# A hybrid decoder trunk on one core: the planner's instruction order tied down by order-only edges

## The chip, the cores and the metric

The kernel runs on one core of one Trainium2 chip. A core has five engines that each work through an instruction stream of their own: PE (TensorE, matrix products; its weight loads are listed apart as PEld), DVE (VectorE), ACT (ScalarE), POOL (GpSimd) and SP (SyncE, which here issues most of the transfers). An engine takes its instructions strictly in the order of its stream; an instruction that has to wait for another engine or for a transfer holds up all that stand behind it. The metric is the device time of one execution in microseconds, the median of several.

## The reference

Two layers over 512 rows of 1024 numbers in float32. Each layer has three sub-layers, each with a normalisation ahead of it and one behind it:

```python
for i in range(2):
    h = rmsnorm(x, mix_pre_g[i])
    z = h @ w_in[i]                    # 1024 -> 3206, split into ten parts
    out_a = spatial_gating(...)        # 4 groups of 64, chunks of 128 rows
    out_b = retention_chunkwise(...)   # 6 heads of 64, rotary
    out_c = forgetting_attention(...)  # 6 heads of 64, blocks of 128 queries
    x = x + rmsnorm(concat(out_a, out_b, out_c) @ w_o[i], mix_post_g[i])

    h = rmsnorm(x, ffn_pre_g[i])
    g = causal_conv3(h @ w_gate[i])    # 1024 -> 4096
    f = (gelu(g) * (h @ w_up[i])) @ w_down[i]
    x = x + rmsnorm(f, ffn_post_g[i])

    gate = sigmoid(rmsnorm(x, ple_pre_g[i]) @ w_ple_gate[i])
    x = x + rmsnorm((p[i] @ w_ple_proj[i]) * gate, ple_post_g[i])
```

## The kernel before

**Products.** Every float32 operand is split into a high and a low part of the matmul type: `split` has ACT copy the high part and DVE subtract it from the source, which gives the low part. A product is then three matmuls (high by high, high by low, low by high; `mm3`). Row-major weights come through `tm_units`: a transfer on SP's queue into `traw`, then the split into `thl` (high and low side by side), two rows of blocks at a time.

**Start of the program.** Chunk 0 of the input `x` (128 rows) is loaded, and `Plain.__call__` prepares it for the products: DVE multiplies each half row by the gain into `h`, PE transposes the four 128x128 blocks of `h` into `hps` (a matmul with `k_ident`), and `split` stores them into `hT`. Then the weights of the projection `uv` are loaded and split, and chunks 1 to 3 are prepared in the same way. The projection takes 24 matmuls of 512 columns for each chunk, 96 in all, from `thl` and `hT` into `ps`. The next projection of the program, `fv`, has 390 columns a chunk, and its `thl` splits are 128x2x390.

**Mixers.** A written order of steps interleaves the three mixers. The last pair of heads of the forgetting attention, `fox_attend(2)`, ends in 10 matmuls `ops<-fet`, whose operand `fet` ACT and DVE copy out of PSUM; the result goes to `cc`. Behind it comes the last retention step and the out projection (`wo`, with weights in `thl` again, and the embedding's operands in `ehl`).

**Feed-forward.** 32 blocks a layer (`gate_up`), each 128 columns of four quarters of the weights. Seven products a block are taken from sums of the weights that DVE builds (`ws`, then the splits `wg`, `wsa`, `wsb`, `wu`); the results collect in the banks `beta` and `ag`, and DVE and ACT combine them in `gs` and `us`. Between these PE takes the matmuls of the down projection (`dn`) of an earlier group of blocks.

**What sets the order.** All calls go through the class `Plan`, which records them first. `issue()` then runs through the recorded program with costs of its own for each instruction, takes on each engine the first recorded one that is ready, and so gets one list, `order`. The instructions are made in that order. In the kernel before, the framework's own scheduler still gets the instructions after that and puts each engine's stream in order by its own rules, with only the true dependences as its limits; the streams that run are therefore not quite the list. All instructions are made at one line, so that every row of the profile has line 404.

Of the kernel before, what the change touches and what calls it, by code (L numbers as in the profile page):

```python
# [49 lines left out]
class Plan:  # L50
# [15 lines left out]
    HOP = {"PE": 197, "DVE": 128, "ACT": 131, "POOL": 80, "SP": 0}  # L66
    HOP_PE = {"PE": 0, "DVE": 250, "ACT": 270, "POOL": 190, "SP": 100}

    def __init__(self):
        self.ops = []  # L70
        self.table = {}
        self.tiles = {}
        self.real = {}
        self.fenced = False
        self.kind = {}
        self.place = {}
        self.scratch = bacc.Bacc("TRN2", target_bir_lowering=False, num_devices=1)
# [143 lines left out]
    def issue(self):  # L221
# [35 lines left out]
        order = []  # L257
# [52 lines left out]
        def unpark(tag, now):  # L310
            q = parked[tag]
            while q:
                other = blocked(q[0])
                if other == tag:
                    return
                i = heapq.heappop(q)
                if other is None:
                    take(i, now)
                else:
                    heapq.heappush(parked[other], i)  # L320

        def complete(i, now):
            nonlocal front
            freed = []
            for t in set(ops[i][5]):
                uses[t] -= 1
                if not uses[t]:
                    tag = self.tiles[t][0]
                    heapq.heappush(slots[tag], now)
                    if t in self.kind:  # L330
                        c, k = self.place[t]
                        heapq.heappush(unused[c], (now, k))
                        freed += [f"b8 {k}" for k in (*self.SETS, None)]
                    freed.append(tag)
            for j in users[i]:
                if ops[j][0] != "PE":
                    release(j, now)
                elif ops[i][0] != "PE":
                    release(j, now + self.HOP_PE[ops[i][0]] - self.HOP[ops[i][0]])
            done[i] = True  # L340
            if i == front:
                while front < n and done[front]:
                    front += 1
                freed = list(parked)
            for tag in freed:
                unpark(tag, now)

        def release(j, now):
            left[j] -= 1
            ready_at[j] = max(ready_at[j], now)  # L350
            if not left[j]:
                offer(j, now)
# [6 lines left out]
        while len(order) < n:  # L359
            progress = False  # L360
            for e in names:
                while waiting[e] and waiting[e][0][0] <= now:
                    _, pr, i = heapq.heappop(waiting[e])
                    heapq.heappush(ready[e], (pr, i))
                if ready[e] and free[e] <= now:
                    _, i = heapq.heappop(ready[e])
                    busy, nbytes = ops[i][6][:2]
                    if e == "PE":
                        if columns.get(now // self.TICK - 1, 0) < self.WARM:
                            busy *= 2  # L370
                        tick = (now + busy) // self.TICK
                        columns[tick] = columns.get(tick, 0) + ops[i][6][2]
                    if self.table.get(i) not in (None, table):
                        table = self.table[i]
                        busy += self.LOAD
                    free[e] = now + busy
                    end = now + busy + self.HOP[e]
                    if nbytes:
                        rate, wait = (215.0, 4500) if e == "POOL" else (340.0, 2600)
                        dma_free = max(dma_free, now + busy) + nbytes / rate  # L380
                        end = dma_free + wait
                    order.append(i)
                    heapq.heappush(finish, (end, i))
                    if e == "PE":
                        for j in users[i]:
                            if ops[j][0] == "PE":
                                release(j, now + busy)
                    progress = True
            if progress:
                continue  # L390
            nxt = [finish[0][0]] if finish else []
            for e in names:
                if ready[e]:
                    nxt.append(free[e])
                elif waiting[e]:
                    nxt.append(max(free[e], waiting[e][0][0]))
            t = min(x for x in nxt)
            now = max(now, t)
            while finish and finish[0][0] <= now:
                _, i = heapq.heappop(finish)  # L400
                complete(i, now)
        for i in order:
            o = ops[i]
            o[1](*[self.map(v) for v in o[2]], **{k: self.map(v) for k, v in o[3].items()})  # L404


def two_pi_parts():
# [66 lines left out]

def body(ctx, tc, a, out):
    nc = tc.nc
    plan = Plan()
    V, A, G, T, SY = (plan.engine(n, e) for n, e in (
        ("DVE", nc.vector), ("ACT", nc.scalar), ("POOL", nc.gpsimd), ("PE", nc.tensor), ("SP", nc.sync)))

# [39 lines left out]
    class Rows:  # L520
        def __init__(self, src):
            self.src, self.t = src, [None, None]
# [782 lines left out]
```

## Time and profile before

| | |
|---|---|
| median of 3 runs | 1635.08 us (1634.15 to 1640.05) |
| the profiled execution's own time | 1635.78 us |
| its span in the profile | 1633.7 us |
| mean granted TensorE clock | 0.995 of full speed |
| busy: PE, DVE, ACT, POOL | 98%, 76%, 51%, 6% of the span |

The own time is the span and 2.1 us around it. A busy share is a mean over the span; stretches with other limits lie inside it. In the views, an instruction's idle time before it is given with the engine whose signal ended it. A group "x24" in a timeline is 24 instructions of the same kind in a row. The three shapes on a row are partitions by elements.

### The profile page before, as it was taken

How to read it: one execution, taken by the hardware profiler on the slowest of the kernel's cores; microseconds unless marked ns; L12 is line 12 of the kernel's file. 1: busy time of each engine (PE TensorE's matmuls, PEld its weight loads, DVE VectorE, ACT ScalarE, POOL GpSimd, SP SyncE). 2: the span in 40 equal slices, each digit the busy share in tenths (PEclk: the TensorE clock that was granted, in tenths of full speed). 3: DMA queues.
4: the chain of work that ended last, by engine and by line, in shares of the span. 5: the costliest groups of instructions: out<-in, count | busy, mean ns of one | idle time of the engine just before them, and what ended most of it. 6: DMA issues, size and time to landing. Idle time of an engine off the chain costs nothing. (4 is left out here: it accounts for less than half of the span.)

```text
span 1633.7 us, 25124 instructions
## 1 busy us (share of the span) xinstructions
PE 1594.8 (98%) x10034; PEld 1409.9 (86%) x10034; DVE 1239.0 (76%) x1949; ACT 840.0 (51%) x1378; POOL 93.7 (6%) x157
## 2 busy tenths in 40 slices
PE   6999999999999999999999999999999999999998
PEld 5887687999999999998888776879999999999987
DVE  6466758988788788786774568599788788788784
ACT  5335626765554554554562346386554554555453
POOL 1000011000000000001230000110000000000022
PEclk8999999999999999999999999999999999999999
DMA  8213216323323324336543033172334233234441
GB/s 295 91 65 104 101 69 228 108 94 114 110 78 124 104 78 129 100 99 261 192 165 104 27 129 121 49 258 78 104 104 129 78 104 129 78 104 130 179 157 65
DMA packets 63421, 197.48 MB, mean 121 GB/s; under 512 B 7348, under 2 KB 15164, under 8 KB 63304
## 3 DMA queue, kind: packets, MB, share of 16 engines
q1 hardware_dynamic: 63160, 195.81, 35.5%
q8 instruction: 79, 1.29, 0.3%
q14 instruction: 38, 0.31, 0.1%
q10 hardware_dynamic: 144, 0.07, 0.0%
HBM read 178.52 MB, written 17.33 MB: 120 GB/s over the span
## 5 line engine op out<-in xcount | busy, mean ns | idle before, releaser
L404 PE MATMUL dn<-thl,act 128*128 128x512 f32 x1536 | 368.0, 390 | 0.0
L404 PEld LDWEIGHTS dn<-thl,act 128*128 128x128 f32 x1536 | 282.8, 188 | 54.0
L404 PE MATMUL ps<-thl,hT 128*128 128x512 f32 (+3 forms) x984 | 206.5, 368 | 0.1
L404 PEld LDWEIGHTS ps<-thl,hT 128*128 128x128 f32 x984 | 177.7, 190 | 22.8 <-ACT hT L404 0.5
L404 DVE TENSOR_TENSOR thl<-traw,thl 128x1024 fp32r<-128x1024 f32 (+2 forms) x120 | 141.2, 1185 | 37.2 <-ACT thl L404 36.4
L404 ACT CAST thl<-traw 128x1024 fp32r<-128x1024 f32 (+2 forms) x120 | 121.0, 1020 | 50.6 <-PE fps L404 10.7
L404 PE MATMUL beta<-hb,wg 128*128 128x256 f32 x768 | 104.7, 281 | 4.6 <-DVE wg L404 4.6
L404 PEld LDWEIGHTS beta<-hb,wg 128*128 128x128 f32 x768 | 100.6, 189 | 9.3 <-DVE wg L404 5.0
L404 ACT COPY gs<-beta 128x256 f32<-128x256 f32 x128 | 47.6, 372 | 111.4 <-PE beta L404 111.3
L404 PE MATMUL ag<-hb,wg 128*128 128x256 f32 x768 | 103.0, 283 | 0.0
L404 PE MATMUL beta<-hh,wsa 128*128 128x256 f32 x768 | 101.7, 282 | 0.5 <-DVE wsa L404 0.2
L404 PE MATMUL beta<-hh,wu 128*128 128x256 f32 x768 | 102.0, 282 | 0.1
L404 PE MATMUL beta<-hh,wsb 128*128 128x256 f32 x768 | 101.8, 281 | 0.0
L404 PE MATMUL ag<-hd,wsa 128*128 128x256 f32 x768 | 100.8, 281 | 0.9 <-DVE gs L404 0.9
L404 PEld LDWEIGHTS beta<-hh,wu 128*128 128x128 f32 x768 | 94.0, 188 | 8.8 <-DVE us L404 7.3
L404 DVE TENSOR_TENSOR wsa<-ws,wsa 128x1024 fp32r<-128x1024 f32 x64 | 78.2, 1221 | 30.8 <-ACT wsa L404 25.7
L404 PE MATMUL ag<-hb,wsb 128*128 128x256 f32 x768 | 100.8, 280 | 0.0
L404 PEld LDWEIGHTS beta<-hh,wsa 128*128 128x128 f32 x768 | 95.4, 190 | 1.4 <-ACT gs L404 0.6
L404 PEld LDWEIGHTS ag<-hb,wg 128*128 128x128 f32 x768 | 96.3, 191 | 0.0
L404 PEld LDWEIGHTS ag<-hd,wsa 128*128 128x128 f32 x768 | 94.8, 189 | 1.7 <-DVE gs L404 1.3
L404 DVE SCALAR_TENSOR_TENSOR cv<-gs,cw,cv 128x511 f32<-128x511 f32 (+1 forms) x128 | 95.4, 745 | 0.9
L404 PEld LDWEIGHTS beta<-hh,wsb 128*128 128x128 f32 x768 | 94.5, 189 | 1.7 <-ACT gs L404 1.2
(194 smaller groups left out, 2709.1 us busy)
## 6 DMA issues: line engine op xcount, KB each, us to landing
graw<-in_w_gu_dram SPq DMA_DIRECT2D x128, 512.0 KB
traw<-in_w_dn_dram SPq DMA_DIRECT2D x64, 512.0 KB
x<-x SPq DMA_DIRECT2D x40, 512.0 KB
fraw<-in_w_fm_dram SPq DMA_DIRECT2D x30, 512.0 KB
traw<-in_w_wo_dram SPq DMA_DIRECT2D x16, 512.0 KB
traw<-in_w_pg_dram SPq DMA_DIRECT2D x16, 512.0 KB
x<-in_x_dram SPq DMA_DIRECT2D x8, 512.0 KB
traw<-in_w_uv_dram SPq DMA_DIRECT2D x8, 512.0 KB
```

Source lines behind the costliest of these rows:

```text
L404: o[1](*[self.map(v) for v in o[2]], **{k: self.map(v) for k, v in o[3].items()})
```

## The change

Every instruction that `issue()` makes gets an order-only edge to the one made before it on the same engine: no semaphore and no wait goes with it, it only binds the framework's scheduler. Each engine's stream is then exactly its part of `order`.

```diff
-    def __init__(self):
+    def __init__(self, tc):
+        self.tc = tc
...
+        newest = {}
         for i in order:
             o = ops[i]
-            o[1](*[self.map(v) for v in o[2]], **{k: self.map(v) for k, v in o[3].items()})
+            made = o[1](*[self.map(v) for v in o[2]], **{k: self.map(v) for k, v in o[3].items()})
+            if o[0] in newest:
+                self.tc.add_manual_dep(made.ins, newest[o[0]], mybir.DependencyInfo(mybir.DependencyClass.NoSync, mybir.DependencyReason.DATA), reason="order of the plan")
+            newest[o[0]] = made.ins.name
...
-    plan = Plan()
+    plan = Plan(tc)
```

The instructions themselves are the same, in number and kind (9774 matmuls and transposes on PE, 1951 rows on DVE, 1260 on ACT, 162 on POOL, 433 on SP). Some 989 of PE's change their place, 1409 of DVE's, 772 of ACT's, 5 of POOL's and 257 of SP's, most by a few places. Three places follow, line 404 being before and line 406 after the change.

The first instructions of DVE's stream, where `h` are the half rows of `x` times the gain, `thl` the low parts of weights (1024 elements for `uv`, 2x390 for `fv`) and `hT` those of the transposed rows. Before:

```order
L404 TENSOR_TENSOR h<-x,gain 128x512 x2
L404 TENSOR_TENSOR thl<-traw,thl 128x1024
L404 TENSOR_TENSOR hT<-hps,hT 128x4x128 x2
L404 TENSOR_TENSOR thl<-traw,thl 128x1024 x3
L404 TENSOR_TENSOR thl<-traw,thl 128x2x390 x2
L404 TENSOR_TENSOR h<-x,gain 128x512 x5
L404 TENSOR_TENSOR hT<-hps,hT 128x4x128 x3
L404 TENSOR_TENSOR h<-x,gain 128x512
```

After:

```order
L406 TENSOR_TENSOR h<-x,gain 128x512 x2
L406 TENSOR_TENSOR thl<-traw,thl 128x1024
L406 TENSOR_TENSOR hT<-hps,hT 128x4x128 x2
L406 TENSOR_TENSOR thl<-traw,thl 128x1024 x3
L406 TENSOR_TENSOR h<-x,gain 128x512 x5
L406 TENSOR_TENSOR hT<-hps,hT 128x4x128 x3
L406 TENSOR_TENSOR h<-x,gain 128x512
```

The two splits of 2x390 no longer stand ahead of the five half rows.

The first instructions of PE's stream, where `hps` are the transposes of half rows (four each) and `ps` the matmuls of `uv` (512 columns) and `fv` (390). Before:

```order
L404 MATMUL hps<-k_ident,h 128x128 x8
L404 MATMUL ps<-thl,hT 128x512 x24
L404 MATMUL hps<-k_ident,h 128x128 x20
L404 MATMUL ps<-thl,hT 128x512 x5
L404 MATMUL hps<-k_ident,h 128x128 x4
L404 MATMUL ps<-thl,hT 128x512 x67
L404 MATMUL ps<-thl,hT 128x390 x17
```

After:

```order
L406 MATMUL hps<-k_ident,h 128x128 x8
L406 MATMUL ps<-thl,hT 128x512 x16
L406 MATMUL hps<-k_ident,h 128x128 x4
L406 MATMUL ps<-thl,hT 128x512
L406 MATMUL hps<-k_ident,h 128x128 x4
L406 MATMUL ps<-thl,hT 128x512
L406 MATMUL hps<-k_ident,h 128x128 x4
L406 MATMUL ps<-thl,hT 128x512
L406 MATMUL hps<-k_ident,h 128x128 x8
L406 MATMUL ps<-thl,hT 128x512 x9
L406 MATMUL hps<-k_ident,h 128x128 x4
L406 MATMUL ps<-thl,hT 128x512 x68
```

The transposes of the chunks 1 to 3 now lie between the matmuls of chunk 0, and the same 96 matmuls of `uv` are cut otherwise.

ACT's stream at the end of the mixers of layer 0, up to the last `fet` that the 10 matmuls `ops` need; `rr` belong to the retention, `thl` is the out projection's weight, `ehl` the embedding's. Before:

```order
L404 ACTIVATE pe,den<-pe,nm 128x512
L404 CAST thl<-traw 128x1024 x2
L404 ACTIVATE pe,den<-pe,nm 128x512
L404 COPY fet<-tps 128x4x128
L404 ACTIVATE rr<-rps 32x512
L404 CAST thl<-traw 128x1024
L404 COPY rr<-rps 32x512
L404 ACTIVATE rr<-rps 32x512
L404 COPY rr<-rps 32x512
L404 CAST thl<-traw 128x1024
L404 COPY fet<-tps 128x4x128
```

After:

```order
L406 ACTIVATE pe,den<-pe,nm 128x512 x2
L406 COPY fet<-tps 128x4x128
L406 ACTIVATE rr<-rps 32x512
L406 COPY rr<-rps 32x512
L406 ACTIVATE rr<-rps 32x512
L406 COPY rr<-rps 32x512
L406 COPY fet<-tps 128x4x128
L406 CAST thl<-traw 128x1024
L406 CAST cc<-ops 128x512
L406 CAST thl<-traw 128x1024 x5
L406 ACTIVATE rsq<-rops 128x512
```

Four casts of `thl` that stood ahead of the last `fet` stand behind it; one is ahead of, five are behind the cast of the result `cc`. On DVE the matching subtractions move the same way (one of them stood behind `cc<-ops` before, five do after). The other layer has the same change.

## Rows read from the trace of the kernel before

**Rows 1.** The page's first part: busy us (share) and instructions of each engine.

```profile
PE 1594.8 (98%) x10034; PEld 1409.9 (86%) x10034; DVE 1239.0 (76%) x1949; ACT 840.0 (51%) x1378; POOL 93.7 (6%) x157
```

**Rows 2.** Windows: us, busy of PE, PEld, DVE, ACT, POOL; granted clock, DMA share, GB/s.

```profile
20.00:25.00 5.00, 0.00 (x0) 0.00 (x0) 2.10 (x3) 2.60 (x4) 0.79 (x2) 0.56 1.05 367
25.00:30.00 5.00, 4.51 (x21) 4.51 (x22) 5.00 (x8) 3.09 (x5) 1.18 (x1) 0.50 1.02 389
215.00:235.00 20.00, 20.00 (x117) 16.55 (x116) 8.60 (x17) 2.72 (x5) 3.81 (x4) 1.00 0.01 4
280.00:285.00 5.00, 5.00 (x32) 5.00 (x31) 5.00 (x8) 2.93 (x6) 0.00 (x0) 0.66 0.93 333
300.00:740.00 440.00, 439.94 (x3125) 410.56 (x3124) 364.29 (x487) 232.02 (x356) 0.00 (x0) 1.00 0.32 105
```

**Rows 3.** Waits of PE: total us, times, longest.

```profile
PE hps L404 <- DVE h L404: 18.7, 10, 7.8
PE beta L404 <- DVE wg L404: 4.6, 2, 2.4
PE ops L404 <- ACT fet L404: 3.8, 2, 2.1
```

**Rows 4.** Timeline of PE from the start: start, us, instructions, [idle before].

```profile
7.80 1.97 PE L404 MATMUL hps<-k_ident,h 128*128 128x128 f32 x8 [7.80 <-DVE h L404]
...
25.49 4.53 PE L404 MATMUL hps<-k_ident,h 128*128 128x128 f32 x20 [7.83 <-DVE h L404]
29.67 1.92 PE L404 MATMUL ps<-thl,hT 128*128 128x512 f32 x5
31.42 0.60 PE L404 MATMUL hps<-k_ident,h 128*128 128x128 f32 x4
31.78 18.49 PE L404 MATMUL ps<-thl,hT 128*128 128x512 f32 x84
```

**Rows 5.** Timeline of DVE from the start.

```profile
11.71 3.48 DVE L404 TENSOR_TENSOR thl<-traw,thl 128x1024 fp32r<-128x1024 f32 x3
22.78 2.06 DVE L404 TENSOR_TENSOR thl<-traw,thl 128x780 fp32r<-128x780 f32 x2 [7.59 <-ACT thl L404]
24.75 3.54 DVE L404 TENSOR_TENSOR h<-x,gain 128x512 f32<-128x512 f32 x5
...
34.90 0.97 DVE L404 TENSOR_TENSOR thl<-traw,thl 128x780 fp32r<-128x780 f32 x1
```

**Rows 6.** Timeline of ACT from the start; junk squares a row that has landed.

```profile
14.62 1.06 ACT L404 ACTIVATE junk<-x 128x1024 bf16<-128x1024 f32 x1
...
19.77 1.05 ACT L404 ACTIVATE junk<-x 128x1024 bf16<-128x1024 f32 x1
...
21.90 0.84 ACT L404 CAST thl<-traw 128x780 fp32r<-128x780 f32 x1 [0.99 <-DMA traw<-in_w_fv_dram]
```

**Rows 7.** Timeline of PE in layer 0's third sub-layer, a run of full matmuls.

```profile
790.06 22.03 PE L404 MATMUL ps<-thl,hT 128*128 128x512 f32 x96
```

**Rows 8.** Timeline of PE at the last attend of layer 0.

```profile
204.38 2.37 PE L404 MATMUL ops<-fet,mix 128*64 128x512 f32 x14 [1.78 <-ACT fet L404]
```

**Rows 9.** Timeline of ACT at the same place.

```profile
195.21 1.98 ACT L404 CAST thl<-traw 128x1024 fp32r<-128x1024 f32 x2
...
202.67 1.04 ACT L404 CAST thl<-traw 128x1024 fp32r<-128x1024 f32 x1
203.74 0.59 ACT L404 COPY fet<-tps 128x512 f32<-128x512 f32 x1
```

**Rows 10.** Timeline of DVE at the start of layer 0's feed-forward.

```profile
267.33 1.22 DVE L404 TENSOR_TENSOR ws<-graw 128x1024 f32<-128x1024 f32 x1
...
280.90 1.22 DVE L404 TENSOR_TENSOR wsa<-ws,wsa 128x1024 fp32r<-128x1024 f32 x1
```

**Rows 11.** Waits of PE's weight loads.

```profile
PEld beta L404 <- DVE us L404: 7.3, 26, 0.4
```

**Rows 12.** Timeline of DVE in a feed-forward block.

```profile
467.69 0.42 DVE L404 SCALAR_TENSOR_TENSOR us<-beta,us 128x256 f32<-128x256 f32 x1
```

## The prediction

> **What bounds the kernel now.** I read the page's first part, then windows, then the waits of PE, then the timelines at the places that these name. PE is busy 98% of the span, 1594.8 of 1633.7 us [rows 1]. In the feed-forward stretch from 300 to 740 us it is busy 439.94 of 440.00 us, with DVE at 364.29, which is 83% [rows 2]. So an order can win only where PE stands still, and the waits of PE show how little that is: 18.7 us for `h`, 4.6 for `wg`, 3.8 for `fet` [rows 3]. Of the 18.7, 7.80 lie ahead of the first transpose and 7.83 ahead of the transposes at 25.49 [rows 4]. The first 7.80 are the loading of the first rows, which no order here moves; the 7.83 are an order's doing, as follows.
>
> **The start: what it gains.** Before the change DVE ends its four `uv` splits at 11.71 + 3.48 = 15.19, then waits 7.59 us for the `fv` splits, whose ACT partner waits for the transfer that lands at 21.90; only behind them does it make the five half rows, from 24.75 [rows 5, 6]. PE is through with 24 matmuls by then and waits for these half rows. They don't need `fv`, and their input was there: ACT squares the first of the rows at 14.62 and the last at 19.77, so that one landed no later than this [rows 6]. The clock falls meanwhile: 0.56 of full speed in 20 to 25 us, 0.50 in 25 to 30 us, which is the lower of the two levels (1.2 GHz) [rows 2].
>
> After the change the half rows follow the `uv` splits at once. Five take 3.54 us [rows 5], so they are done at 15.19 + 3.54 = 18.73, and the transposes that need them, interleaved with chunk 0's matmuls, at about 19.2 (0.5 for the last four and the signal between the engines, an estimate from 0.60 for four [rows 4]). By the listing 77 of the 96 `uv` matmuls and four transposes are then left. A matmul at full clock is 22.03 / 96 = 0.229 us [rows 7], four transposes 31.78 − 31.42 = 0.36 [rows 4]: 77 × 0.229 + 0.36 = 18.0, so `uv` ends at 19.2 + 18.0 = 37.2. Before, 67 `uv` matmuls were left at 31.78 [rows 4]: 31.78 + 67 × 0.229 = 47.1. The gain is **9.9 us**.
>
> Its bounds. Above: the whole wait and the half clock are gone, 7.83 + (31.78 − 25.49 − 24 × 0.09 − 5 × 0.229 = 3.0) = 10.8. Below: the last row lands only at 19.77, so that its half rows end near 19.77 + 0.71 = 20.5 instead of 18.73 (−1.75), and a stretch at lower clock remains. The trace has such a stretch elsewhere, 280 to 285 us at 0.66, which costs 5 × (1 − 0.66) = 1.7 [rows 2]. 9.9 − 1.75 − 1.7 = 6.4.
>
> Does anything eat it? The `fv` splits move behind the half rows: the first two can be cast from 21.90 on [rows 6]. In the trace of before the last of the low parts is through at 34.90 + 0.97 = 35.9 [rows 5], so that even unmoved it would be there before PE first wants it at 37.2; by the new order it comes some 5 us earlier, as DVE is through with the half rows 6 us sooner. Were it late, PE would lose what is late. On SP's queue two loads move behind stores that wait for DVE's results (the second half of the retention's value weights behind the stores of the rotary tables, a weight of the next fox projection behind those of the running sums). By the listing PE has more than 40 matmuls between such a store's place and the first use of the weights, over 9 us at 0.229; I cost that at nothing, and a load that comes too late costs its lateness. The next waits of PE of any size lie at 204 us and behind it [rows 3, 8], so the start's gain carries on whole.
>
> **The last attend of each layer.** PE waits 1.78 us in layer 0 for `fet` [rows 8], and 3.8 in both layers [rows 3], so the other is 2.06. ACT's row before that `fet` is a `thl` cast of 1.04, and two of 1.98 and one more stood earlier on [rows 9]; all four go behind it in the change. The last cast alone is 1.04 a layer, 2.1 in both, and as `fet` begins that much earlier it is the least that I see as sure; the whole of the waits is 3.84, since the retention's `rr` copies are freed too. The middle is **3.0**; the bounds are 0 (the `rr` copies wait for PE and `fet` is held as before) and 3.84. PE's matmuls around it stand as they did.
>
> **The start of the feed-forward, each layer.** PE waits 4.6 us for `wg` at two places [rows 3], on a chain that DVE sets. Of the DVE rows ahead of it, one `ws` sum of 1.22 stood among the half rows at 267.33; after the change it stands between `wg` and `wsa` [rows 10]. So `wg` comes 1.22 earlier and `wsa` no earlier; what PE gains on the one it may wait for on the other. I take 0. Bounds, both layers: 2 × 1.22 = 2.4 lost, where `wsa` is late by as much as was moved, and 2.4 gained, where it is not waited for.
>
> **The rest of the feed-forward.** In the order listing the loads of `wu` stand directly behind the products of `wsb` in 30 of 64 blocks, where 16 did before; a filler matmul of `dn` stood between in the others. That exposes them to `us`. But `us`, which stood right behind the split of `wsa` on DVE in 38 blocks and now does in 14, mostly comes ahead of it. PE's loads waited 7.3 us in all for `us`, 26 times, at most 0.4 [rows 11], and its matmuls did not stand still for it (439.94 of 440.00 busy [rows 2]). The two moves go against each other: 0, with bounds of 7.3 gained at the most (all those waits gone, if they had reached the matmuls) and, as a loss, what rival 3 below works out.
>
> **The sum** is made against the profiled execution's own time, 1635.78, which is 0.7 above the median: 1635.78 − 9.9 − 3.0 + 0 + 0 = **1622.9**, say 1623. The best of the bounds without the feed-forward's 7.3 is 1635.78 − 10.8 − 3.84 − 2.4 = 1618.7, the worst 1635.78 − 6.4 − 0 + 2.4 = 1631.8. Half of one per cent, 8.2 us, is about what a measurement here can tell from no change.
>
> **Rivals.**
>
> 1. *The clock stays low behind the transposes.* From 16 to 19 us PE now has 16 transposes and few long matmuls, and in the trace the window of 25 to 30 us, with 20 transposes in it, shows 0.50 and no rise [rows 2, 4]. If the clock falls for one or two stretches of 1.7 us each, the sum is 1624.6 to 1626.3. Against it: PE is not idle ahead of them. The Trainium skill says of "TensorE: Matmul & The Clock Gate", section "Part 4: PE-mode transpose", that the full clock does not come on for transposes, since they do not count as busy time in the same way; the row at 0.50 agrees, but its stretch also had an idle one ahead of it, so the row can't part the two. By that rule the time would be that of this rival.
>
> 2. *The late casts hold up the out projection.* Behind `cc`, DVE now has four more `thl` subtractions a layer than before. If each of 1.22 us (the size of those of 1024 elements in [rows 10]) delays PE, that is 4 × 1.22 = 4.9 a layer and 9.8 in both: 1622.9 + 9.8 = 1632.7, no change by my measure. It decides the sign only with the start's gain small. Against it: DVE is busy only 8.60 of the 20 us that follow (215 to 235 us) while PE is saturated [rows 2], so there is room for 4.9 and more.
>
> 3. *Slower: the fixed order makes PE wait in the feed-forward.* The framework's order had seen to it that a matmul that can't start lets another pass; the list goes by costs of its own, and where an instruction takes longer than those, a whole stream waits. The place is `wu` behind `wsb`, where a `dn` matmul was the cover. To be slower by 0.5% it needs 12.9 + 8.2 = 21.1 us over 64 blocks, 0.33 a block; the waits now are 7.3 / 64 = 0.11 [rows 11]. One `us` of 0.42 [rows 12] added to every block gives 64 × 0.42 = 27: 1622.9 + 27 = 1650. Against it: DVE has 17% to spare in this stretch, and `us` is moved ahead of `wsa` in most blocks.
>
> **How the numbers follow.** The forecast (the start and the attend gain, the rest is even) has 0.63 and its own range is 1618 to 1628; rival 1 has 0.12, rival 2 0.17, rival 3 0.08. The predicted time is the forecast's, 1623. The range goes down to 1616, since some of the 7.3 us of loads' waits may turn into time, and up to 1636, to take in rival 2 with the lower bound of the start; rival 3 is left out. Faster by over 0.5% means under 1626.9: nearly all of the forecast, and half of rival 1, 0.67 in all. Within 0.5% are the other half of rival 1 and rival 2 for the most part, 0.22. Slower: rival 3, and a mishap of rivals 2 and 3 together, 0.11.
>
> **What would show it.** Start: no gap of PE between 16 and 25 us, a clock of 1.0 in 20 to 30 us, and the first `fv` matmul (390 columns) near 37 us. If the gap stays at half its size, the rows of `x` were late. Attend: the wait of `ops` for `fet` at under 1 us in all, and no new wait of `wo` or `rops` behind it (rival 2). Feed-forward: 300 to 740 us with PE as saturated as before, and the loads' wait for `us` no longer than 7.3; if it has grown to 20 or more, rival 3 holds. A time above 1632 with the start's gap gone would mean that the feed-forward lost what the start won.

## The result and the profile after

The changed kernel takes 1619.86 us (median of 4, 1619.01 to 1620.10); the kernel before took 1636.64 beside it (1634.15 to 1640.05). The ratio is 0.9895 with a 95% interval of 0.9875 to 0.9916: faster by 1.05%, inside the range of 1616 to 1636 and 3 us below the forecast of 1623. The profiled execution has a span of 1617.6 against 1633.7 and a granted clock of 0.999. The sum of the prediction is right in its first term; the others came out as different numbers that added up to more.

The page's first part of the changed kernel, to be read beside [rows 1]: the counts of instructions are the same, and PE is busy 8.7 us less. Part of that is the clock: the 20 transposes that took 4.53 us at the lower level [rows 4] take 2.34 at the full one (run e5 below).

```profile
PE 1586.1 (98%) x10034; PEld 1406.1 (87%) x10034; DVE 1232.9 (76%) x1949; ACT 833.7 (52%) x1378; POOL 98.7 (6%) x157
```

PE's timeline from the start, beside [rows 4]:

```profile
9.90 6.75 PE L406 MATMUL ps<-thl,hT 128*128 128x512 f32 x16
16.48 0.60 PE L406 MATMUL hps<-k_ident,h 128*128 128x128 f32 x4
...
21.45 0.60 PE L406 MATMUL hps<-k_ident,h 128*128 128x128 f32 x4
21.81 18.74 PE L406 MATMUL ps<-thl,hT 128*128 128x512 f32 x85
40.38 0.60 PE L406 MATMUL rbps<-k_ident,rs 128*128 128x128 f32 x4
```

Behind the first 7.8 us no idle time in brackets is left. By the listing 68 of the 85 are `uv` matmuls, so the first `fv` matmul starts at 21.81 + 68 × 0.229 = 37.4. The small transposes `rbps`, which stand among the `fv` matmuls, start at 40.38; they started at 50.10 before.

Three windows of the changed kernel, beside the first two and the last of [rows 2] (us, busy of PE, PEld, DVE, ACT, POOL; clock, DMA share, GB/s):

```profile
20.00:25.00 5.00, 5.00 (x26) 4.10 (x25) 4.70 (x10) 4.97 (x10) 1.09 (x2) 1.00 1.04 369
25.00:30.00 5.00, 5.00 (x24) 4.15 (x23) 5.00 (x7) 4.20 (x7) 1.17 (x1) 1.00 1.03 389
300.00:740.00 440.00, 440.00 (x3105) 411.28 (x3105) 359.55 (x482) 229.41 (x353) 0.00 (x0) 1.00 0.34 115
```

The clock is at its full level (2.4 GHz) where it was at 0.56 and 0.50. The feed-forward is as saturated as before.

The waits of PE in the changed kernel, beside [rows 3] (total us, times, longest), and one of its weight loads, beside [rows 11]:

```profile
PE hps L406 <- DVE h L406: 13.0, 12, 7.8
PE cps L406 <- DVE ro L406: 4.0, 6, 1.4
PE beta L406 <- DVE wg L406: 3.1, 2, 1.6
PE beta L406 <- ACT gs L406: 2.4, 2, 1.2
...
PEld beta L406 <- DVE us L406: 2.4, 12, 0.3
```

Of the 18.7 for `h` the start's 7.8 behind the first transposes are gone, but 2 us of small new ones have come. The wait of `ops` for `fet` is gone altogether. In its place stands a wait that the trace of before does not have: `cps`, the transposes of the retention's output, for `ro`.

Where the 16.1 us between the two spans' last matmuls come from is read from PE's timelines: the start of the same matmuls in both, and how the difference grows from one to the next.

| stretch of PE's timeline | layer 0 | layer 1 |
|---|---|---|
| up to `rbps` (start of the program) | 50.10 to 40.38: −9.7 | |
| `rbps` to the first `wo` (mixers) | −2.0 | −1.7 |
| first `wo` to the last `ops` (last attend) | −2.1 | −2.4 |
| last `ops` to the first `beta` (out projection, embedding) | +3.1 | +3.1 |
| first `beta` to the first `dn` (feed-forward's start) | −1.1 | −0.3 |
| first to last `dn` (the rest of the feed-forward) | −2.3 | −1.9 |
| last `dn` to `rbps` of layer 1, or to the end | +1.5 | −0.2 |

The start's 9.7 stand as forecast (9.9). The last attend's gain is larger than the 3.0 in the sum, and more than all of it is lost again right behind. A little of both is bookkeeping: one `wo` matmul of 0.23 us a layer stood ahead of the last `ops` before and stands behind it now, so that the attend really gains 4.0 in the two layers together and the stretch behind it loses 2.8 in each. The feed-forward, costed at 0, brings 5.6 in both layers; the mixers, not costed, 3.7.

### The profile page after: what moved, and what is told of

Read it like the earlier page. It is cut to its first block, busy times and chain, and to the rows that moved or that the text cites. A ratio compares the mean times of both kernels' runs of the same rounds, so it can differ in the third digit from the quotient of the medians.

```text
span 1617.6 us, 25075 instructions
## 1 busy us (share of the span) xinstructions
PE 1586.1 (98%) x10034; PEld 1406.1 (87%) x10034; DVE 1232.9 (76%) x1949; ACT 833.7 (52%) x1378; POOL 98.7 (6%) x157
## 4 chain that ended last, share of the span: by engine, by line
PE 87%; DVE 6%; ACT 3%; POOL 2%; issue 1%; DMA 0%; SPq 0%; POOLq 0%; DVEq 0%; ACTq 0%
PE beta L406 22%; PE dn L406 20%; PE ag L406 17%; PE ps L406 12%; PE fps L406 4%; PE rps L406 4%; PE gps L406 2%; PE wo L406 1%; ACT junk L406 1%; DVE x L406 1%; PE ops L406 1%; POOL y L406 1%; PE sps L406 1%; PE hps L406 1%; PE tps L406 1%
## 5 line engine op out<-in xcount | busy, mean ns | idle before, releaser
L406 DVE TENSOR_TENSOR facc<-dn,facc 128x512 f32<-128x512 f32 x112 | 77.2, 690 | 27.5 <-PE dn L406 26.4
```

The costliest lines, as they stand in the source:

```text
L406: made = o[1](*[self.map(v) for v in o[2]], **{k: self.map(v) for k, v in o[3].items()})
```

## The experiments

All but the last four leave the plan's list as it is and give the edges to only a part of it; `pos` is the place in the list. The diffs show the condition alone; where it names `pos`, the loop above it reads `for pos, i in enumerate(order):`. The kernel before ran beside each.

| run | edges, list | us (median) | ratio to before (95%) |
|---|---|---|---|
| e1_start_dve | DVE, start | 1633.81 | 0.9990 (0.9981 to 1.0000) |
| e5_start_dve_act | DVE and ACT, start | 1627.37 | 0.9949 (0.9934 to 0.9964) |
| e2_all_but_start | all engines, all but the start | 1629.02 | 0.9960 (0.9946 to 0.9974) |
| e3_ffn_only | all engines, feed-forward | 1631.47 | 0.9976 (0.9967 to 0.9985) |
| e4_dve_only | DVE | 1634.77 | 0.9994 (0.9985 to 1.0004) |
| e7_pe_only | PE | 1656.76 | 1.0128 (1.0113 to 1.0143) |
| e8_dve_act | DVE and ACT | 1617.85 | 0.9888 (0.9871 to 0.9904) |
| e6_tidy | all, list changed | 1615.81 | 0.9878 (0.9863 to 0.9892) |
| e9_tidy_pe_free | all but PE, list of e6 | 1616.29 | 0.9881 (0.9861 to 0.9900) |
| e10_beside | all, `ehl` beside POOL | 1618.59 | 0.9894 (0.9878 to 0.9910) |
| e11_kt_beside | all, `kt` beside POOL | 1615.34 | 0.9874 (0.9858 to 0.9889) |

### The start

**e1_start_dve.**

```diff
-            if o[0] in newest:
+            if o[0] in newest and o[0] == "DVE" and pos < 188:
```

> Only DVE's first 31 instructions keep the edges; PE's order is then the framework's, 20 transposes in one piece behind 24 matmuls. Theory A (the two early fv splits on DVE alone made the start's wait): the start's whole gain is there, the first fv matmul near 37 us, and the time is 1635.8 - 9.7 = 1626. Rival B (it takes the transposes between the matmuls on PE as well, since 20 in one piece drop the clock): half of the gain or less, 1631 or more, with a granted clock well under 1.0 in 20 to 25 us.

It took 1633.81 us, 1.7 less than the kernel before. The time is one that rival B allows, but its cause isn't there: PE's 20 transposes ran at full clock, and a wait had changed its place. From the timelines of DVE, ACT and PE in this run, and two of its windows:

```profile
15.13 3.10 DVE L406 TENSOR_TENSOR h<-x,gain 128x512 f32<-128x512 f32 x5
25.42 1.89 DVE L406 TENSOR_TENSOR hT<-hps,hT 128x512 fp32r<-128x512 f32 x3 [7.19 <-ACT hT L406]
24.06 0.84 ACT L406 CAST thl<-traw 128x780 fp32r<-128x780 f32 x1 [0.24 <-DMA traw<-in_w_fv_dram]
24.81 2.53 ACT L406 CAST hT<-hps 128x512 fp32r<-128x512 f32 x5
17.85 2.34 PE L406 MATMUL hps<-k_ident,h 128*128 128x128 f32 x20
25.44 2.50 PE L406 MATMUL ps<-thl,hT 128*128 128x512 f32 x5 [5.24 <-ACT hT L406]
15.00:20.00 5.00, 5.00 (x34) 4.40 (x32) 3.23 (x6) 2.65 (x5) 2.80 (x4) 1.00 0.83 245
25.00:30.00 5.00, 4.45 (x12) 3.23 (x13) 4.51 (x9) 4.01 (x8) 0.65 (x1) 0.50 1.01 394
```

DVE makes the half rows at 15.13 and PE transposes them at 17.85, as foreseen. But the copies of the high parts into `hT` stand behind three casts for `fv` in ACT's stream, and these wait for the transfers until 24.06. The `fv` work stood ahead of the rows on two queues; the prediction had looked at DVE's and did not mention these copies of ACT.

**e5_start_dve_act.**

```diff
-            if o[0] in newest:
+            if o[0] in newest and o[0] in ("DVE", "ACT") and pos < 246:
```

> As the first run, but the edges also hold ACT in the start (DVE's and ACT's instructions ahead of the first fv matmul in the list); PE keeps its 20 transposes in one piece. Theory A2 (the fv work stood ahead of the rows on two queues, and DVE's freed half rows met ACT's, whose copies into hT stood behind three fv casts until 24.81): the whole 9.7 is back, 1635.5 - 9.7 = 1626, and no wait of PE for hT over 0.5. Rival B2 (PE's order is needed too, for the clock): 1629 or more, with a clock under 0.9 in 20 to 25 us.

1627.37 us, 9.3 less than the kernel before beside it: theory A2. PE's timeline and two windows of this run:

```profile
17.77 2.34 PE L406 MATMUL hps<-k_ident,h 128*128 128x128 f32 x20
19.87 1.42 PE L406 MATMUL ps<-thl,hT 128*128 128x512 f32 x5
21.65 0.63 PE L406 MATMUL hps<-k_ident,h 128*128 128x128 f32 x4 [0.37 <-DVE h L406]
22.04 18.49 PE L406 MATMUL ps<-thl,hT 128*128 128x512 f32 x84
40.36 0.60 PE L406 MATMUL rbps<-k_ident,rs 128*128 128x128 f32 x4
15.00:20.00 5.00, 5.00 (x34) 4.44 (x33) 4.13 (x8) 2.28 (x6) 2.73 (x4) 1.00 0.88 241
20.00:25.00 5.00, 4.63 (x24) 3.60 (x23) 4.77 (x10) 4.97 (x9) 0.00 (x0) 1.00 1.05 368
```

`rbps` starts at 40.36, as in the changed kernel (40.38). So the two queues together hold the whole of the start's gain, and PE's transposes need not be spread: 20 in one piece, with no idle time ahead of them, run at full clock.

**e2_all_but_start.**

```diff
-            if o[0] in newest:
+            if o[0] in newest and pos >= 246:
```

> The edges begin only with the first fv matmul of the list; the start is the framework's. Theory A (the start and the rest add up): the wait of 7.8 us is back, the rest keeps its 6.4, and the time is 1619.9 + 9.7 = 1629.6. Rival B (the earlier start also sets what comes later): more than 1632, the rest worth less than 4 by itself.

1629.02: theory A. The start and the rest add up (9.2 above the changed kernel's 1619.86).

### The rest: which engines

**e3_ffn_only.**

```diff
-            if o[0] in newest:
+            if o[0] in newest and (1556 <= pos <= 6422 or 8256 <= pos <= 13122):
```

> Edges only from the end of the out projection to the last matmul of the feed-forward, in both layers. Theory A (the order in the feed-forward is worth what the two traces differ by there, 11.20 to 14.19 and 14.17 to 15.87, 4.7 in all): 1631, and the weight loads' wait for us falls from 7.3 to some 2.4 us. Rival B (it is the mixers' order, which sets what DVE has finished when the blocks begin): within 1.5 of the kernel before.

1631.47, 4.1 below the kernel before, and the weight loads' wait for `us` at 2.8: theory A. The profiled execution took 1633.34, and its span is only 2.4 below that of before: at the last attend of layer 0, which has no edges here, its clock fell, which the last section comes back to.

**e4_dve_only** and **e7_pe_only**: edges on one engine all through.

```diff
-            if o[0] in newest:
+            if o[0] in newest and o[0] == "DVE":
```

> Edges on DVE's stream alone; the other four engines are as the framework orders them. Theory A (DVE's order is the cause of start and feed-forward): the start's 9.7 and some 4 of the feed-forward, 1621 to 1623. Rival B (an order of DVE that the others don't follow costs new waits): slower than 1626, which is the start alone.

```diff
-            if o[0] in newest:
+            if o[0] in newest and o[0] == "PE":
```

> Edges on PE's stream alone. Theory A (PE only follows; the gains are those of DVE and ACT): PE reaches the first late half row after 16 matmuls instead of 24, waits to the same 25.4, and has 8 x 0.229 = 1.8 more to do then: 1637, the rest even. Rival B (PE's order makes the framework order the others in step): under 1632.

DVE alone: 1634.77, not told from the kernel before. Its wait for `us` did fall, to 3.0, which is the order of DVE's own work, and from the first to the last `dn` it is 2.2 and 1.6 us shorter than before, nearly as the changed kernel is. But the start waits for ACT as in e1 (4.6 us of `ps` for `hT`), and the trace loses 1.9 behind the last attend of either layer, 0.7 and 1.4 at the start of the feed-forward and 2.0 behind that of layer 0. PE alone: 1656.76, the slowest kernel of all, where 1637 was expected. The start is as expected (`rbps` at 51.84, +1.7); that the rest would be even was wrong. Its waits, and one of them in the timeline:

```profile
PE hps L406 <- DVE h L406: 26.8, 14, 9.7
PE ops L406 <- ACT fet L406: 5.4, 2, 2.7
PE beta L406 <- DVE wg L406: 4.3, 2, 2.2
PE beta L406 <- ACT gs L406: 4.0, 5, 1.4
PE beta L406 <- DVE us L406: 2.8, 14, 0.3
...
PEld beta L406 <- DVE us L406: 9.5, 28, 0.5
...
836.94 1.11 PE L406 MATMUL hps<-k_ident,h 128*128 128x128 f32 x4 [2.94 <-DVE h L406]
```

Those that [rows 3, 11] have are longer here, but for the one for `wg`, and PE's own waits for `gs` and `us` are new: PE goes by one order and those who feed it by another. Behind the 2.94 us for `h` at 836.94 the clock falls as well, to 0.66 in the window from 835 to 845 us. The third sub-layer of layer 0, where this lies, loses 7.1 of the trace's 19.7 us, more than any other stretch; between the first and the last `dn` both layers together lose 4.3.

**e8_dve_act.**

```diff
-            if o[0] in newest:
+            if o[0] in newest and o[0] in ("DVE", "ACT"):
```

> Edges on DVE and ACT all through, PE, POOL and SP by the framework. Theory A2 (the start needs these two; of the rest DVE alone lost what ACT's other order gave back, 2.6 us of cps for ro and a wsa wait of 1.4 among it): the 9.7 of the start and 2 to 4 of the rest, 1622 to 1624. Rival B (each stream out of step with the list costs its own waits): 1626 or more, the start's gain and nothing else.

1617.85, 4 us or more below the better theory. DVE alone brought 0.8, which its interval does not tell from nothing; together with ACT it carries the whole gain. PE's stream, which cost 20 us when it was tied alone, needs no edges behind these two. Against the changed kernel the trace of e8 loses only 1.9 a layer instead of 3.1 behind the last attend, and is 0.5 and 0.7 us worse at the start of the feed-forward.

### The new wait behind the last attend

In the changed kernel, at the place of `cps`: two rows of DVE, two of POOL, two of PE.

```profile
203.56 2.35 DVE L406 TENSOR_TENSOR thl<-traw,thl 128x1024 fp32r<-128x1024 f32 x2
207.47 0.69 DVE L406 TENSOR_TENSOR ro<-rops,y 128x512 f32<-128x512 f32 x1 [1.56 <-POOL y L406]
203.73 1.14 POOL L406 TENSOR_SCALAR vh<-ss 128x8 f32<-128x8 f32 x1 [40.57 <-DVE ss L406]
204.96 2.48 POOL L406 TENSOR_TENSOR y<-vh,minus_half 128x8 f32<-128x8 f32 x1
202.25 4.60 PE L406 MATMUL wo<-thl,cc 128*128 128x512 f32 x19
208.21 0.66 PE L406 MATMUL cps<-k_ident,ro 128*128 128x128 f32 x4 [1.36 <-DVE ro L406]
```

`ro` waits for `y`, so it was not DVE's queue that was late: the two subtractions were through 1.56 us earlier. POOL's two tiny instructions took 1.14 and 2.48 us. The second retention step of the same layer has 0.24 and 1.67, with nothing of DVE beside it; so has the kernel before at both places. That is 1.71 us on a chain that PE waits for at its end.

**e6_tidy**: two subtractions go ahead of that place in the list. The numbers are places in the record, the same 6700 later for the other layer: 1526 and 1528 are `thl` subtractions, 1527 the ACT cast between them, 1375 `qd`, 1556 and 1558 those of `ehl`, 1405 the second `ro`.

```diff
         newest = {}
+        for d in (0, 6700):
+            for i, behind in ((1526, 1375), (1527, 1526), (1528, 1527), (1556, 1405), (1558, 1556)):
+                order.remove(i + d)
+                order.insert(order.index(behind + d) + 1, i + d)
```

> All edges, but in the list of each layer two subtractions of thl, which ran on DVE beside POOL's two small instructions for the retention's norm, move some 7 us ahead (behind qd), and the two of ehl behind the next ro. Theory A (beside 128x1024 subtractions POOL took 1.14 and 2.48 us for these instead of 0.24 and 1.67, and the second ss stood 0.5 behind ehl; both reach PE as the wait of cps for ro, 4.0 us in both layers): that wait falls under 1 us and the time by 3 to 4, to 1616 to 1617. Rival B (the late ro comes from the retention's chain being taken earlier, whatever DVE does beside it): POOL's 1.14 and 2.48 stay or go without effect, and the time stays within 1 of 1619.9.

1615.81, 4.0 below the changed kernel: theory A. It moves two pairs of subtractions at once, and what each is worth was not parted. POOL and the wait in this run:

```profile
204.07 0.24 POOL L410 TENSOR_SCALAR vh<-ss 128x8 f32<-128x8 f32 x1 [40.69 <-DVE ss L410]
204.39 1.67 POOL L410 TENSOR_TENSOR y<-vh,minus_half 128x8 f32<-128x8 f32 x1
PE cps L410 <- DVE ro L410: 0.4, 2, 0.2
```

**e10_beside** and **e11_kt_beside** put something else beside POOL: the subtractions of `ehl`, or the scalings `kt` (1373 and 1374; 1349 is `ss`, 1348 the `rsq` ahead of it; 1555 and 1557, ACT's casts of `ehl`, move along and stand behind `rsq` on ACT, where the trace of e6 has them too).

```diff
-            ... (1556, 1405), (1558, 1556)):
+            ... (1555, 1348), (1557, 1555), (1556, 1349), (1558, 1556)):
```

> The list of e6_tidy, but the two subtractions of ehl stand right behind the first ss of each layer, where those of thl stood in the changed kernel. Theory A (POOL is slowed by what DVE runs beside it, whoever needs that): vh 1.14 and y 2.48 again at the first ss, the wait of cps for ro back at 1 to 2 a layer, and 1615.8 + 3 = 1619. Rival B (the wait came from the thl subtractions' own place in the chain): vh 0.24 and y 1.67, and within 1 of 1615.8.

```diff
-            ... (1556, 1405), (1558, 1556)):
+            ... (1556, 1405), (1558, 1556), (1373, 1349), (1374, 1373)):
```

> The list of e6_tidy, but two scalings kt of 128x192, which read PSUM and a column of scalars, stand right behind the first ss, so that DVE is busy with them while POOL runs vh and the beginning of y. Theory A (only operations that read two tensors of SBUF hold POOL up): vh stays at 0.24, y at 1.67, the time within 0.7 of 1615.8. Rival B (any DVE work beside POOL slows it): vh near 0.6 or more and the time up by 0.7 to 1.5.

Both went as theory A has it: 1618.59 and 1615.34. First e10, then e11, from the timelines of DVE and POOL:

```profile
203.69 2.35 DVE L410 TENSOR_TENSOR ehl<-eraw,ehl 128x1024 fp32r<-128x1024 f32 x2
203.86 1.14 POOL L410 TENSOR_SCALAR vh<-ss 128x8 f32<-128x8 f32 x1 [40.66 <-DVE ss L410]
205.09 2.48 POOL L410 TENSOR_TENSOR y<-vh,minus_half 128x8 f32<-128x8 f32 x1
PE cps L410 <- DVE ro L410: 3.3, 4, 1.5
```

```profile
202.92 0.73 DVE L410 TENSOR_SCALAR kt<-kps,k_kdec 128x192 f32<-128x192 f32 x2
203.09 0.24 POOL L410 TENSOR_SCALAR vh<-ss 128x8 f32<-128x8 f32 x1 [40.29 <-DVE ss L410]
203.42 1.67 POOL L410 TENSOR_TENSOR y<-vh,minus_half 128x8 f32<-128x8 f32 x1
```

Other subtractions of the same kind do the same to POOL, to the hundredth; the scalings, which read PSUM, do nothing to it, though DVE is busy with them for all of `vh` and 0.24 us of `y`. They are also shorter, 0.73 us for two against 2.35, so that e11 does not part the place of the operand from the kind and length of the work.

**e9_tidy_pe_free**: the list of e6, and no edge on PE.

```diff
-            if o[0] in newest:
+            if o[0] in newest and o[0] != "PE":
```

> The list of e6_tidy with edges on every engine but PE. Theory A (the two gains add: 4.0 of the moved subtractions, 2.0 that PE brought where the framework orders it behind DVE and ACT): 1615.8 - 2.0 = 1613.8. Rival B (both take the same waits away, cps for ro above all): 1615 to 1616.

1616.29, as e6: rival B. The 2.0 us by which e8 was ahead of the changed kernel don't come on top of the moved subtractions: most of them were the smaller wait of `cps` for `ro` (2.7 in e8 and 4.0 in the changed kernel, 0.4 in e6 and 0.2 in e9). Of the versions tried, e11's has the lowest median, 1615.34, and e6 and e9 stand within a microsecond of it, about as far apart as one kernel's runs are.

## Why the prediction was right, point by point

- **The start (9.9 forecast, 9.7 measured).** The size held: no wait, full clock, `fv` at 37.4 where 37.2 was forecast. Of the mechanism the prediction had half: e1 showed that DVE's order alone brings 1.7, and e5 that DVE's and ACT's bring all. The change moves both, so the number was right; that ACT's half came with it was luck. Two readings of the first microseconds were off, without effect on the sum: ACT's first square of the late rows begins at 13.38 and not at 14.62, and what ends the first 7.8 us is not the rows, which ACT reads from 4.50 on, but the gain, as DVE's first row in the trace of before shows. No run moved that load.

```profile
7.06 1.29 DVE L404 TENSOR_TENSOR h<-x,gain 128x512 f32<-128x512 f32 x2 [7.06 <-DMA gain<-in_mix_pre_g_dram]
```

- **Rival 1, the clock behind the transposes: wrong.** The changed kernel has 1.00 from 20 to 30 us, and e5 has 1.00 with 20 transposes in one piece. In e1 the transposes have 1.00 too, and only the window from 25 to 30 us, behind a wait of 5.24, shows 0.50 again. What the lower clock of [rows 2] went with was the idle time ahead. The rule of the Trainium skill quoted there ("TensorE: Matmul & The Clock Gate", "Part 4: PE-mode transpose") did not decide here: 20 transposes in one piece, 2.1 us from first to last, did not lower a clock that was at its full level.
- **The last attend (3.0 forecast, 4.0 measured).** The waits of `ops` for `fet` are gone, and the stretch is 2.1 and 2.4 shorter, 4.5 in all. Without the `wo` matmul that left it in each layer that is 4.0: the upper bound of 3.84, the whole of the waits, and not the middle.
- **Rival 2, the late casts: right in kind.** Its price was 9.8 by DVE's queue; the stretch behind the attend did lose 3.1 a layer. But DVE had room, as the prediction said. The subtractions held up POOL instead, and with it `ro`; of the 3.1 a layer e6 gets back a little over half (from the last `ops` to the first `beta` it loses 1.4 and 1.3). In the changed kernel's timeline the 3.1 are 2.1 ahead of `cps`, 0.5 ahead of `hps`, 0.23 for the matmul that moved in, and the rest between `wo` matmuls; e6 takes away the 2.1 and loses 0.4 more between those.
- **The feed-forward (0 forecast, −5.6 measured).** This is the mis-sized term. The loads' waits for `us` fell from 7.3 to 2.4, and the time from the first to the last `dn` fell with them, by 2.3 and 1.9: the prediction had taken them as hidden, since PE showed as saturated, and had kept the 7.3 only as an outer bound. The traces of the runs bear it out, with both layers together: 903.6 to 904.6 us where the loads wait 7.3 to 7.6 (before, e1, e5), 899.9 to 900.8 where they wait 2.3 to 3.0 (the changed kernel, e2, e3, e4, e6, e8), 908.9 in e7 with 9.5 and 2.8 of PE's own. e3 shows that the order within the feed-forward is what counts (1631.47), e4 that DVE's is enough for this part. At the feed-forward's start PE waited 2.28 us for `wg` in layer 0, with a stretch at 0.66 behind it [rows 2]; now it waits less for `wg` but also for ACT's `gs`, which the prediction had not seen, and the clock stays at 1.00 there. In layer 1, where the clock had not fallen before, the gain is only 0.3. PE in layer 0 of the changed kernel:

```profile
266.93 1.42 PE L406 MATMUL beta<-hb,wg 128*128 128x256 f32 x10 [1.56 <-DVE wg L406]
...
270.91 0.50 PE L406 MATMUL beta<-hh,wsa 128*128 128x256 f32 x2 [1.20 <-ACT gs L406]
```

- **Rival 3, waits in the feed-forward: not here.** The loads' waits for `us` fell instead of growing. In e7, where PE alone was tied, they did grow, to 9.5 in 28 waits, but the feed-forward from first to last `dn` lost only 4.3 of the 20 us; most of that loss lies at other places. In the changed kernel, where the other engines are tied too, the same stretches are 4.2 shorter.
- **Not in the sum:** 3.7 gained in the mixers, and 1.5 lost behind the feed-forward of layer 0, in small waits of `hps` for `h`. They were read from the timelines, and no run was made for them. The mixers gain 1.7 to 2.1 a layer in e2, e6 and e8 as well, but 0.1 and 1.0 with DVE alone (e4); the 1.5 behind the feed-forward are 1.4 in e8 and 2.0 in e4.

So 9.7 of the 16.1 came from the step that was worked out, and the remaining 6.4, against 3.0 forecast, is what smaller terms of both signs left: gains of some 13.8 and losses of some 7.4, most of which the prediction had at nothing. That they came out near the forecast is in part luck.

## What to carry to other kernels

When an instruction waits at the head of one queue, look for the same work at the head of the others: freeing one of two queues gives almost nothing (1.7 of 9.7 here). In this kernel an order paid only where the engines that feed each other kept it together: tied on one alone it ran from no gain (DVE, whose shorter feed-forward was eaten by new waits) to 20 us lost (PE). And a PE that shows as saturated can still lose time to small waits of its weight loads: with 4.9 us of them gone, the feed-forward took 4.2 us less.

## What the runs showed of the hardware

- **POOL beside DVE.** `vh` and `y` (128x8) take 0.24 and 1.67 us alone and 1.14 and 2.48 beside 128x1024 subtractions, the same in the changed kernel, e2, e4, e8 and e10. `vh` ends about 0.1 us behind the first of the subtractions (203.73 + 1.14 = 204.87, against 203.56 + 1.22 = 204.78). Beside `kt`, which is shorter and has one operand in PSUM, nothing changes (e11). The Trainium skill states a mechanism that fits ("SBUF — State Buffer", "SBUF: two separate sides"): DVE and GpSimd share a pair of ports under an exclusive lock, which a DVE operation with two inputs in SBUF takes against a GpSimd operation that reads SBUF. The runs agree with it; that the lock is the cause they don't show.
- **The clock after an idle stretch.** Waits of 7.83 (before) and 5.24 us (e1) left PE at 0.50 in the window behind them, that of 2.28 at 0.66, while one of 2.35 us at the same place of the other layer left it at 1.00. Two waits of about the same length can end differently, and at one place from run to run: `ops` waits 1.78 us for `fet` in the trace of before and its 14 matmuls then take 2.37 [rows 8]; in e3, behind 1.92, the clock is 0.66 from 204 to 209 us and they take 4.06, 1.7 us more:

```profile
204.50 4.06 PE L406 MATMUL ops<-fet,mix 128*64 128x512 f32 x14 [1.92 <-ACT fet L406]
204.00:209.00 5.00, 4.50 (x16) 2.61 (x17) 3.68 (x7) 1.01 (x2) 0.00 (x0) 0.66 0.42 173
```
